# Hybrid encoder layer: memory queries and half of the SSD gate of the first token group made feature-major by seven products

## The chip, the cores and the metric

The kernel runs on one core of a Trainium2 chip. The metric is the device time of one execution in microseconds (us); lower is better. Before the change it is 1805.97 us, the median of 3 runs (1805.81 to 1807.87).

## The reference, cut to what matters

One layer of an encoder runs over 1280 tokens (1024 of a sample, 256 of a prompt), 2048 features wide, in fp32.

```python
hn = rms_norm(x, norm_g)
proj = hn @ w_in                                   # 2048 -> 4896 columns
xbc, z_ssd, dt_raw, q, k, v, z_att, mq, z_mem = split_cols(proj, IN_SIZES)
...
y = (y_f + y_b + d_skip[:, None] * xs)             # SSD, forward and backward
yg = (y * silu(z_ssd)).reshape(b, T, 2, 512)       # the SSD gate, two groups of 512 columns
o_ssd = rms_norm(yg, ...)
...
mq = rms_norm(mq.reshape(b, T, 4, 128), mq_norm_g) # memory queries, 4 heads of 128
sm = einsum('bthd,bmhd->bhtm', mq, mk) * 128 ** -0.5
o_mem = einsum('bhtm,bmhd->bthd', softmax(sm), mv) * silu(z_mem)
...
return x + concat([o_ssd, o_att, o_mem]) @ w_out
```

## The kernel before, in words

Tokens go in tiles of 128; tiles 0 to 4 are the first group (640 tokens), tiles 5 to 9 the second. Every large product is made in three matmuls: both operands are split into a high and a low fp32r part (`xH`/`xL` of the activations, `wh`/`wl` of the weights, `wsplit`, lines 200 to 204: ScalarE makes `wh`, VectorE `wl`), and high*high, high*low and low*high are summed in PSUM.

There are three forms of a large product:

- `block_tok` (lines 230 to 262) makes 512 columns **token-major** (tokens on partitions): for each of 16 slices k of the 2048 features, 5 token tiles with 3 matmuls of 512 columns each, 240 matmuls in all.
- `block_feat` (lines 264 to 298) makes 256 columns **feature-major** (columns on partitions): 192 matmuls of 320 tokens.
- `block_pair` (lines 1167 to 1198) makes 256 columns feature-major by a scheme of **seven products** of half-size blocks in place of eight: 7 products times 8 slices times 3 parts, 168 matmuls of 320 tokens. GpSimd forms the weights' sums ahead (`weight_sums`, line 1164, four operations per slice), ScalarE and VectorE split weights and sums, and `ev_seven` (lines 1264 to 1297) adds the seven results up. A unit is one such block of 256 columns.

The program runs in this order: memory keys and values; the attention queries `q` of group one; the **stage of seven products** with ten units for group one (gate of the attention `za`, gate of the memory part `zm`, and the six blocks x0 to x5 that feed the convolution); then `kv`, `mq`, `z0`, `z1` of group one, token-major; then everything of group two (x0 to x4, kv, x5, q, za, z0, z1, mq, zm); then the output product, first token-major for group one, then eight seven-product units for group two.

The many small pieces (norms, attention `attn`, memory attention `mem_attn`, the SSD passes `ssd_up` and `ssd_down`) are generators in two **lanes**. `run` (lines 1354 to 1376) drives a large product slice by slice; after each slice `pump` takes some steps off each lane, at the two rates that `RATES` (lines 32 to 34) gives for that block (for a feature-major block half of them, since its slices are half as long). A step stands in the program behind the slice at which it was taken. `need(fn, tiles)` runs a lane on at once until the named pieces are done. The leftovers of the seven products (taps of the convolution, gates) wait in the list `left`, and are taken by `some_left`.

What the change touches: `mem_attn` (lines 697 to 785) loads the queries `mq` of a tile, squares them (line 705), transposes them on TensorE into the PSUM tile `pmq` (line 713), splits the transposed ones (715, 717), and goes on to scores (`pms`, 730), transposes of the weights (`pmt`, 752) and values (`pmo`, 767). `ssd_down` (lines 991 to 1048) loads the gate `z` of a tile (line 1006), takes the part from the state (`pyb`, line 1022), multiplies by the gate (line 1026), and squares into the gate's own tile (line 1027); `turn_ssd` (line 986) transposes an earlier result into `pr`. `x_stats` and `stage_stats` sum the squares of the input rows. All small PSUM tiles share one ring of three, `mix`.

Of the kernel before, what the change touches and what calls it, by code (L numbers as in the profile page):

```python
# [19 lines left out]
P = 128  # L20
# [11 lines left out]
RATES = ({'kv': (2.0, 1.0), 'mq': (2.4, 1.6), 'z0': (2.2, 1.7), 'z1': (2.2, 1.7)},  # L32
         {'kv': (1.2, 1.5), 'x': (1.75, 1.85), 'q': (1.6, 2.5), 'za': (1.6, 2.5), 'z0': (1.55, 2.6),
          'z1': (1.55, 2.65), 'mq': (1.55, 2.8), 'zm': (1.55, 2.85), 'o': (1.95, 1.9)})
FAR = 1e30

UNITS = (0, 4, 1, 5, 2, 6, 7, 3, 8, 9)
# [6 lines left out]
def hymba_encoder_kernel(  # L44
# [62 lines left out]
    zT_d = [[dram([P, 4, 640], f"zT{c}_{g}") for g in range(2)] for c in range(2)]  # L107
    q_d = [dram([P, 512], f"q_{t}") for t in range(NT)]
    mq_d = [dram([P, 512], f"mq_{t}") for t in range(NT)]
    k_d = [dram([P, P], f"k_{t}") for t in range(NT)]  # L110
# [586 lines left out]
    def mem_attn(t):  # L697
# [4 lines left out]
        S.dma_start(q, mq_d[t])  # L702
        yield
        sq = w2("sq")
        A.activation(sq, q, AF.Square)
# [5 lines left out]
        ps = psum("pmq")  # L711
        for h in range(4):
            T.transpose(ps[:, h * P:(h + 1) * P].bitcast(F32R), qr[:, h * P:(h + 1) * P], identr)
# [3 lines left out]
        V.tensor_sub(ql, ps, qh.bitcast(F32))  # L717
# [273 lines left out]
    def ssd_down(t):  # L991
# [8 lines left out]
        for g in range(2):  # L1000
            c = slice(g * 512, (g + 1) * 512)

            y = mp.tile([P, 512], F32, tag="ya" if t % 2 else "rf", name="yd", bufs=2)
            S.dma_start(y, yp_d[t][:, c])
            z = mp.tile([P, 512], F32, tag="xs", name="zd", bufs=2)
            S.dma_start(z, z_d[g][t])
# [10 lines left out]
        for g in range(2):  # L1017
            c = slice(g * 512, (g + 1) * 512)
            y, z, st = ld[g]
            if not last:  # L1020
# [12 lines left out]
            if g == 0:  # L1033
                yield
# [229 lines left out]
    def ev_seven(kind, f0):  # L1264

        work, o = (conv_left, 2) if kind is None else (gate_left, 0)
# [35 lines left out]
    def gate_left(c, f0, rs):  # L1302
        th = []

        def tanhs():
            for r in rs:
                th.append(ev.tile([P, 640], F32, tag="evt", name="th"))
                A.activation(th[-1], r[:, :640], AF.Tanh, scale=0.5)

        def last(i):  # L1310
            V.scalar_tensor_tensor(out=th[i], in0=th[i], scalar=1.0, in1=rs[i][:, :640], op0=ALU.add, op1=ALU.mult)
            S.dma_start(zT_d[c][0][:, f0 + i, :], th[i])
        return [tanhs, lambda: last(0), lambda: last(1)]
# [27 lines left out]
    def x_stats(grp):  # L1341
        if grp == 0:
            yield from stats([(xrow(t), t) for t in range(5)],
                             lambda i: ev.tile([P, 512], F32, tag="evt" if i % 2 else "evu", name="xst"))
        else:
            yield from stats([(xrow(t), t) for t in (8, 9)],
                             lambda i: mp.tile([P, 512], F32, tag="xs" if i % 2 else "ya", name="xst", bufs=2))

    def stage_stats():

        yield from stats([(mrow(i), 10 + i) for i in range(4)] + [(xrow(t), t) for t in (5, 6, 7)],
# [127 lines left out]
    units = [(i // 2, i % 2 * 2) if i < 4 else (None, 2 * (i - 4)) for i in UNITS]  # L1479
# [44 lines left out]
    queue(1, x_stats, [1])  # L1524
# [30 lines left out]
    for b in range(5):  # L1555
        feat("x", b, ev_conv(1, 2 * b), 1, extra=one_left)
    need(attn, range(4))
    kv_shift()
    run(block_tok(w_kv, 5, ev_dtkv(5)), RATES[1]["kv"], extra=one_left)
    queue(0, k_prep, range(5, 10))  # L1560
    queue(0, attn, [4])
    queue(1, dt_prep, [5])
    feat("x", 5, ev_conv(1, 10), 1, extra=one_left)
# [3 lines left out]

    run(block_tok(w_in_rows("q"), 5, ev_raw(q_d, 5)), RATES[1]["q"], extra=when_done(2, lambda: queue(1, ssd_up, range(4, 8))))
# [108 lines left out]
```

## Time and profile before

| what | value |
|---|---|
| median of 3 runs | 1805.97 us |
| the profiled execution's own time | 1804.94 us |
| its span in the trace | 1803.2 us |
| TensorE matmul busy | 1791.4 us, 99% of the span |
| VectorE busy | 1210.3 us, 67% |
| ScalarE busy | 902.3 us, 50% |
| GpSimd busy | 456.6 us, 25% |
| granted TensorE clock | 1.0 |

The span is what lies between the first and the last instruction; 1.7 us of the execution lie around it. Matmuls overlap in the profile: a matmul's own duration is longer than the distance to the next one, so the sum of durations says nothing about what a matmul costs. The distance from start to start does.

### The profile page before, as it was taken

What the parts mean: (1) busy time and instruction counts of PE and PEld (TensorE: products, weight loads), DVE (VectorE), ACT (ScalarE), POOL (GpSimd) and SP (SyncE); (2) the same over time, 40 slices, a digit from 0 to 9 for tenths busy, and PEclk for the clock granted to TensorE, in tenths of its full rate; (3) what the DMA queues carried; (4) which work ended last, traced back from release to release, by engine and by line L of the source; (5) the groups of instructions that cost most, each with busy time, mean ns of one, the idle gap of its engine ahead of it and who ended that gap; (6) DMA issues with size and microseconds to landing.
All of it is one profiled execution on the core that took longest, in us unless ns stands there. A gap on an engine that the chain in (4) does not pass through costs nothing.

```text
span 1803.2 us, 30420 instructions
## 1 busy us (share of the span) xinstructions
PE 1791.4 (99%) x10546; PEld 1607.0 (89%) x10546; DVE 1210.3 (67%) x2303; ACT 902.3 (50%) x1999; POOL 456.6 (25%) x772
## 2 busy tenths in 40 slices
PE   9999999999999999999999999999999999999999
PEld 8789999999887799999989988887898888899999
DVE  5595788877657877675755766556775653867665
ACT  6554455444445756464435645544474533543332
POOL 0105888861110000000000001101100000058775
PEclk9999999999999999999999999999999999999999
DMA  8654454446544544344336355457785554644442
GB/s 299 190 178 122 137 151 152 126 134 217 168 134 152 177 133 139 121 132 133 118 95 192 113 164 173 128 181 233 230 269 162 180 189 142 215 154 147 141 144 79
DMA packets 198891, 290.58 MB, mean 161 GB/s; under 512 B 18960, under 2 KB 80464, under 8 KB 198736
## 3 DMA queue, kind: packets, MB, share of 16 engines
q1 hardware_dynamic: 198592, 288.57, 51.4%
q8 instruction: 83, 1.36, 0.3%
q14 instruction: 72, 0.59, 0.1%
q10 hardware_dynamic: 144, 0.06, 0.0%
HBM read 231.12 MB, written 57.44 MB: 160 GB/s over the span
## 4 chain that ended last, share of the span: by engine, by line
PE 87%; issue 5%; DMA 3%; DVE 2%; ACT 1%; POOL 1%; SPq 0%; ACTq 0%; DVEq 0%; POOLq 0%
PE acc L254 13%; PE acc L256 13%; PE acc L255 12%; PE acc L1194 6%; PE acc L1192 6%; PE acc L1193 6%; PE acc L289 5%; PE acc L290 4%; PE acc L291 4%; PE accm L1193 2%; PE accm L1192 2%; PE accm L1194 2%; PE py L924 2%; PE po L667 1%; PE ppt L657 1%
## 5 line engine op out<-in xcount | busy, mean ns | idle before, releaser
L203 DVE TENSOR_TENSOR wl<-wraw,wh 128x512 fp32r<-128x512 f32 (+1 forms) x480 | 340.5, 711 | 273.8 <-ACT wh L202 265.0
L254 PE MATMUL acc<-wh,xH 128*128 128x512 f32 (+1 forms) x1248 | 482.7, 387 | 0.2 <-ACT wh L202 0.2
L255 PE MATMUL acc<-wl,xH 128*128 128x512 f32 (+1 forms) x1248 | 472.2, 378 | 0.6 <-DVE wl L203 0.4
L256 PE MATMUL acc<-wh,xL 128*128 128x512 f32 (+1 forms) x1248 | 472.4, 379 | 0.0
L202 ACT ACTIVATE wh<-wraw 128x512 fp32r<-128x512 f32 (+1 forms) x480 | 293.4, 615 | 348.4 <-PE acc L256 189.5
L255 PEld LDWEIGHTS acc<-wl,xH 128*128 128x128 f32 x1248 | 234.9, 188 | 43.7 <-DVE wl L203 2.8
L254 PEld LDWEIGHTS acc<-wh,xH 128*128 128x128 f32 x1248 | 234.7, 188 | 43.6 <-issue 3.9
L256 PEld LDWEIGHTS acc<-wh,xL 128*128 128x128 f32 x1248 | 234.2, 188 | 43.4
L289 PE MATMUL acc<-xH,wh 128*128 128x320 f32 x640 | 203.9, 319 | 0.0
L290 PE MATMUL acc<-xL,wh 128*128 128x320 f32 x640 | 198.2, 310 | 0.0
L291 PE MATMUL acc<-xH,wl 128*128 128x320 f32 x640 | 198.0, 309 | 0.0
L202 ACT ACTIVATE sh<-ws 128x384 fp32r<-128x384 f32 x144 | 74.9, 525 | 180.9 <-POOL ws L1164 98.5
L203 DVE TENSOR_TENSOR sl<-ws,sh 128x384 fp32r<-128x384 f32 x144 | 100.1, 699 | 93.6 <-ACT sh L202 93.4
L1164 POOL TENSOR_TENSOR ws<-wraw 128x128 f32<-128x128 f32 x144 | 88.9, 617 | 202.5 <-DMA wraw<-in_w_in_pairs_dram 88.1
L629 POOL COPY lg<-nsink 128x2 f32<-128x2 f32 x40 | 16.5, 416 | 436.4 <-PE ppt L657 212.2
L289 PEld LDWEIGHTS acc<-xH,wh 128*128 128x128 f32 x640 | 120.3, 188 | 3.5 <-issue 2.7
L290 PEld LDWEIGHTS acc<-xL,wh 128*128 128x128 f32 x640 | 120.3, 188 | 2.3 <-issue 1.9
L291 PEld LDWEIGHTS acc<-xH,wl 128*128 128x128 f32 x640 | 120.2, 188 | 0.1
L1164 POOL TENSOR_TENSOR ws<-wraw,ws 128x128 f32<-128x128 f32 x144 | 94.6, 657 | 11.3
L358 DVE SCALAR_TENSOR_TENSOR c<-u,vec,c 128x638 f32<-128x638 f32 (+1 forms) x96 | 88.9, 931 | 11.2 <-ACT c L353 10.8
L1164 POOL TENSOR_TENSOR ws<-ws,wraw 128x128 f32<-128x128 f32 x144 | 93.3, 648 | 0.0
L1164 POOL TENSOR_TENSOR wraw<-wraw 128x128 f32<-128x128 f32 x144 | 89.1, 618 | 11.1
(426 smaller groups left out, 3601.3 us busy)
## 6 DMA issues: line engine op xcount, KB each, us to landing
wraw<-in_w_in_laid_dram SPq DMA_DIRECT2D x208, 256.0 KB, 2.8
wraw<-in_w_in_pairs_dram SPq DMA_DIRECT2D x80, 256.0 KB, 2.7
wraw<-in_w_out_laid_dram SPq DMA_DIRECT2D x64, 256.0 KB, 3.1
wraw<-in_w_out_pairs_dram SPq DMA_DIRECT2D x64, 256.0 KB, 2.8
rf<-ac SPq DMA_DIRECT2D x40, 256.0 KB, 3.6
rb<-ac SPq DMA_DIRECT2D x40, 256.0 KB, 4.0
wraw<-in_w_mem_laid_dram SPq DMA_DIRECT2D x32, 256.0 KB, 4.2
xst<-in_x_sample_dram SPq DMA_DIRECT2D x20, 256.0 KB, 4.9
```

The source lines that it names most:

```text
L202: a = A.activation(h, raw, AF.Copy)
L203: b = V.tensor_sub(l, raw, h.bitcast(F32))
L254: T.matmul(ps[t][:, :n], sh, h[:, :n], start=(k_ == 0), stop=False)
L255: T.matmul(ps[t][:, :n], sh, l[:, :n], start=False, stop=False)
L256: T.matmul(ps[t][:, :n], sl, h[:, :n], start=False, stop=(k_ == KT - 1))
L289: T.matmul(o, sh, cur["H", q][:, m, c], start=(k == 0), stop=False)
L290: T.matmul(o, sh, cur["L", q][:, m, c], start=False, stop=False)
L291: T.matmul(o, sl, cur["H", q][:, m, c], start=False, stop=(k == KT - 1))
L1164: G.tensor_tensor(out=o, in0=x, in1=y, op=op)
L1192: T.matmul(ps[p], h, xh, start=(k_ == 0), stop=False)
L1193: T.matmul(ps[p], h, xl, start=False, stop=False)
L1194: T.matmul(ps[p], l, xh, start=False, stop=(k_ == 7))
```

## The change

In words:

- Four more units go through the stage of seven products: y0 and y1, which are the two halves of `z0` (the SSD gate's first 512 columns), and m0 and m1, the two halves of `mq`, all for group one. The stage has 14 units now, in the order za0 x0 za1 x1 zm0 x2 zm1 x3 y0 x4 y1 x5 m0 m1. Their results are stored feature-major, in `yT` and `mT`.
- The token-major blocks `mq` and `z0` of group one are gone. Between the stage and group two stand `kv` and `z1` alone.
- `mem_attn` of tiles 0 to 4 loads a feature-major tile and turns it at its first step; it squares out of PSUM. The split then reads the loaded tile. The number of transposes is the same.
- `ssd_down` of tiles 0 to 4 loads the gate of the first 512 columns feature-major, and turns it with four transposes into the PSUM tile `pz`, which the multiplication reads and the square overwrites.
- The row sums of tiles 8 and 9 are taken in the stage of seven products.
- kv of group two comes after x5, not between x4 and x5; `mem_attn` of group one is queued before `z1`; the rates are new. In words of lane 0: z1 of group one 3.0 (before 2.2), x 2.1 (1.75), kv 1.4 (1.2), q 2.2 (1.6), za 2.05 (1.6), z0 2.0 (1.55), z1, mq and zm 1.9 (1.55); `o` is unchanged.

Core of the diff:

```diff
-RATES = ({'kv': (2.0, 1.0), 'mq': (2.4, 1.6), 'z0': (2.2, 1.7), 'z1': (2.2, 1.7)},
+RATES = ({'kv': (2.0, 1.0), 'z1': (3.0, 1.6)},
...
-UNITS = (0, 4, 1, 5, 2, 6, 7, 3, 8, 9)
+UNITS = (0, 8, 1, 9, 2, 10, 3, 11, 4, 12, 5, 13, 6, 7)
+PAIRS = ('za0', 'za1', 'zm0', 'zm1', 'y0', 'y1', 'm0', 'm1', 'x0', 'x1', 'x2', 'x3', 'x4', 'x5')
...
-        S.dma_start(q, mq_d[t])
-        yield
+        if grp == 0:
+            S.dma_start(hv(q, 4), mT_d[:, :, tc_])
+        else:
+            S.dma_start(q, mq_d[t])
+        yield
+
+        def turned():
+            ps = psum("pmq")
+            for h in range(4):
+                T.transpose(ps[:, h * P:(h + 1) * P].bitcast(F32R), qr[:, h * P:(h + 1) * P], identr)
+            return ps
+
+        tok_ = turned() if grp == 0 else q
         sq = w2("sq")
-        A.activation(sq, q, AF.Square)
+        A.activation(sq, tok_, AF.Square)
...
+        feat_ = q if grp == 0 else turned()
         qh = mp.tile([P, 512], F32R, tag="qT", name="mqh", bufs=2)
-        A.activation(qh, ps, AF.Copy)
+        A.activation(qh, feat_, AF.Copy)
...
+            if g == 0 and t < 5:
+                zr, z = z, psum("pz")
+                for j in range(4):
+                    T.transpose(z[:, j * P:(j + 1) * P].bitcast(F32R), zr[:, j * P:(j + 1) * P], identr)
...
+    def turned_left(dst, f0, rs):
+        def store():
+            for i in range(2):
+                S.dma_start(dst[:, f0 + i, :], rs[i][:, :640])
+        return [store]
...
-    run(block_tok(w_in_rows("mq"), 5, ev_raw(mq_d, 0)), RATES[0]["mq"],
+    queue(0, mem_attn, range(5))
+    run(block_tok(w_in_rows("z1"), 5, ev_gate(1, 0)), RATES[0]["z1"], refill_x(1),
         extra=when_done(1, lambda: queue(1, ssd_up, range(4))))
-    queue(0, mem_attn, range(5))
-    tok("z0", w_in_rows("z0"), ev_gate(0, 0))
-    tok("z1", w_in_rows("z1"), ev_gate(1, 0), refill_x(1))
...
-    for b in range(5):
+    for b in range(6):
         feat("x", b, ev_conv(1, 2 * b), 1, extra=one_left)
```

How it moves instructions on TensorE, at three places. The names: `ppt`, `po` are the transposed weights and the values of the attention, `py`, `pst`, `pyf` products of the SSD, `lg` the attention's weights, `acc` a large product.

First, the end of the attention of tile 3. Before, at the end of x2, the last six of its transposes stand alone behind a run of large matmuls, and the `po` that reads them follows after the 48 large matmuls that begin with the last two rows shown:

```order
L291 MATMUL acc<-xH_7170,wl 128x320
L657 MATMUL ppt<-identr,lg 128x128 x6
L924 MATMUL py<-xs,rb 128x64 x8
L289 MATMUL acc<-xH_7482,wh 128x320
L290 MATMUL acc<-xL_7483,wh 128x320
```

Now it stands at the start of kv of group two, where `need(attn, ...)` runs the lane to its end:

```order
L660 MATMUL ppt<-identr,lg 128x128 x9
L257 MATMUL acc<-wh,xH_6765 128x288
L660 MATMUL ppt<-identr,lg 128x128 x3
L862 MATMUL pst<-bh,bth 128x512
L863 MATMUL pst<-bl,bth 128x512
L864 MATMUL pst<-bh,btl 128x512
L879 MATMUL pyf<-state,bc 128x512
L670 MATMUL po<-pT,v_all 64x256 x6
```

Twelve transposes, a state product and the values now follow each other with one large matmul among them.

Second, the start of the memory attention of a tile. Before (tile 1, in x4), the transposes come a step after the square, which ScalarE took from the loaded tile:

```order
L850 MATMUL pst<-bh,bth 128x512
L851 MATMUL pst<-bl,bth 128x512
L852 MATMUL pst<-bh,btl 128x512
L713 MATMUL pmq<-identr,mq 128x128 x4
L289 MATMUL acc<-xH_6767,wh 128x320
```

Now (tile 0, in kv of group two) they are the first work on the loaded tile:

```order
L862 MATMUL pst<-fh,bth 128x512
L863 MATMUL pst<-fl,bth 128x512
L864 MATMUL pst<-fh,btl 128x512
L714 MATMUL pmq<-identr,mq 128x128 x4
L257 MATMUL acc<-wh,xH_6765 128x288
```

TensorE's row is the same; what it waits for is the load itself, no longer a load that ScalarE has already used.

Third, the backward SSD pass, at a tile of group one. Before, `pyb` opens the work on a tile:

```order
L667 MATMUL po<-pT,v_all 64x256 x4
L1022 MATMUL pyb<-state,cc 128x512
L986 MATMUL pr<-identr,yd 128x128 x4
L291 MATMUL acc<-xH_6933,wl 128x320
L289 MATMUL acc<-xH_6933,wh 128x320
```

Now the gate's transposes stand ahead of it:

```order
L259 MATMUL acc<-wh,xL_7087 128x512
L1039 MATMUL pz<-identr,zd 128x128 x4
L1042 MATMUL pyb<-state,cc 128x512
L998 MATMUL pr<-identr,yd 128x128 x4
L257 MATMUL acc<-wh,xH_7403 128x512
```

Four transposes and one more tile of the PSUM ring have come in, for each of five tiles.

More of the change, by code (lines that the diff above doesn't have):

```diff
@@ L1264, in ev_seven @@
     def ev_seven(kind, f0):
-        work, o = (conv_left, 2) if kind is None else (gate_left, 0)
+        work, o = (conv_left, 2) if kind is None else (turned_left if kind is mT_d else gate_left, 0)
         def begin(u):
@@ L1339, in stats, with x_stats @@
                 yield
[L1341 to L1347, printed above, removed]
+    def x_stats(_):
+        yield from stats([(xrow(t), t) for t in range(5)],
+                         lambda i: ev.tile([P, 512], F32, tag="evt" if i % 2 else "evu", name="xst"))
     def stage_stats():
-        yield from stats([(mrow(i), 10 + i) for i in range(4)] + [(xrow(t), t) for t in (5, 6, 7)],
+        yield from stats([(mrow(i), 10 + i) for i in range(4)] + [(xrow(t), t) for t in range(5, 10)],
                          lambda i: fin.tile([P, 512], F32, tag="xst", name="sst"), ahead=1, group=3)
@@ L1477, in hymba_encoder_kernel @@
         extra=lambda k: p_step(16 + k))
[L1479 removed]
+    dests = (zT_d[0][0], zT_d[1][0], yT_d, mT_d)
+    units = [(dests[i // 2], i % 2 * 2) if i < 8 else (None, 2 * (i - 8)) for i in UNITS]
     squares = stage_stats()
@@ L1553, in one_left, with gate @@
             some_left()
-    for b in range(5):
+    for b in range(6):
         feat("x", b, ev_conv(1, 2 * b), 1, extra=one_left)
+    def gate(name, c, after=None):
+        for b in range(2):
+            feat(name, b, ev_gateT(c, 1, 2 * b), 1, after if b else None)
     need(attn, range(4))
     kv_shift()
-    run(block_tok(w_kv, 5, ev_dtkv(5)), RATES[1]["kv"], extra=one_left)
+    run(block_tok(w_kv, 5, ev_dtkv(5)), RATES[1]["kv"], extra=lambda k: some_left() if left else None)
     queue(0, k_prep, range(5, 10))
```

35 lines of the change are left out of this document (17 added, 18 removed).

## The prediction

> **What bounds the kernel now.** I read the page first, then the chain that ended last, then TensorE's waits, then the stretches on both sides of the place that changes.
>
> ```profile
> span 1803.2 us, 30420 instructions
> ...
> PE 1791.4 (99%) x10546; PEld 1607.0 (89%) x10546; DVE 1210.3 (67%) x2303; ACT 902.3 (50%) x1999; POOL 456.6 (25%) x772
> ...
> PE 87%; issue 5%; DMA 3%; DVE 2%; ACT 1%; POOL 1%; SPq 0%; ACTq 0%; DVEq 0%; POOLq 0%
> ```
>
> TensorE is busy for 99% of the span and makes up 87% of the chain; no other engine is above 67%. A busy share of overlapping matmuls could still hide waits, so the waits come next (engine, what waited, for what: us in all, times, longest).
>
> ```profile
> PE pmt L752 <- DVE mpr L744: 1.5, 2, 0.9
> PE warm L1458 <- DVE zero L1456: 1.3, 1, 1.3
> PE psc L635 <- ACT qT L619: 1.0, 1, 1.0
> PE acc L1194 <- DVE wl L203: 0.9, 2, 0.6
> PE ppt L657 <- DVE nm L637: 0.8, 2, 0.5
> PE pxs L843 <- ACT pT L658: 0.6, 1, 0.6
> PE po L667 <- ACT pT L658: 0.6, 1, 0.6
> PE acc L255 <- DVE wl L203: 0.4, 2, 0.2
> PE acc L1192 <- ACT qs L322: 0.3, 1, 0.3
> PE acc L254 <- ACT wh L202: 0.2, 1, 0.2
> ```
>
> All of TensorE's waits come to 7.6 us, and those in the lanes' work (pmt, psc, ppt, pxs, po) to 4.5. So the time is the sum of what TensorE is given, in every stage. A change of its work counts one for one, as long as the other engines keep up. Next, the stretches (width; then busy us of PE, PEld, DVE, ACT, POOL; granted clock; DMA share; GB/s): the stage of seven products, then kv with mq of group one, then z0 with z1, then x0 to x4.
>
> ```profile
> 155.00:395.00 240.00, 239.08 (x1633) 238.45 (x1633) 193.43 (x291) 124.27 (x248) 200.63 (x310) 1.00 0.45 136
> ```
> ```profile
> 399.40:492.00 92.60, 92.60 (x535) 82.29 (x534) 62.53 (x138) 38.23 (x88) 12.36 (x29) 1.00 0.60 189
> 492.00:632.00 140.00, 138.90 (x697) 112.49 (x695) 99.08 (x207) 84.14 (x209) 13.99 (x25) 1.00 0.52 157
> 632.00:822.00 190.00, 189.08 (x1314) 180.24 (x1314) 134.75 (x289) 108.99 (x258) 9.06 (x15) 1.00 0.43 132
> ```
>
> The clock is 1.00 throughout. In the stage of seven products VectorE is at 81% and GpSimd at 84%: covered, with some 4 us in 24 to spare. Behind it VectorE is at 68%, 71% and 71%.
>
> **The change, term by term.** First the two blocks that go. Token-major matmuls of 512 columns, start to start:
>
> ```profile
> 119.76 0.39 PE L254 MATMUL acc<-wh,xH 128*128 128x512 f32 x1
> ...
> 121.12 0.39 PE L254 MATMUL acc<-wh,xH 128*128 128x512 f32 x1
> ```
>
> Six steps lie between these rows: 1.36 / 6 = 0.2267 us each. Two blocks of 240 matmuls: 480 x 0.2267 = **-108.8 us**.
>
> The four units that come. The first result of each unit is copied out at one and the same place of the unit, so the distance of these copies is the whole period of a unit, its waits and its edges included:
>
> ```profile
> L1282 ACT ACTIVATE yu<-acc x10: 417/430/439, 171.8 to 394.4; 128x320 f32<-128x320 f32 x10
> ```
>
> 222.6 us over nine periods is 24.73 us a unit. Four units: **+98.9 us**. With 168 matmuls that is 0.147 us each; a 320-column matmul costs 0.46 us per thousand columns against 0.44 of the 512-column one, so the shape is a little dearer, and the saved eighth outweighs it. The cover holds: GpSimd's 20.7 us and VectorE's 19.9 us per 24.7 us unit (84% and 81%) are those of the mixture that stands there already, and the new units need less of VectorE than a convolution unit (no taps).
>
> [...]
>
> The turning of the gate: 20 transposes. The transposes of the memory queries are of the same kind (row of the first, and of what starts behind it):
>
> ```profile
> 753.55 0.49 PE L713 MATMUL pmq<-identr,mq 128*128 128x128 f32 x4
> 753.87 0.51 PE L843 MATMUL pxs<-identr,xc 128*128 128x128 f32 x4
> ```
>
> 0.32 us for four: five times that is **+1.6 us**. The queries' own transposes only change their place. TensorE's work is thus -108.8 + 98.9 + 1.6 = **-8.3 us**.
>
> Edits at nothing: 32 slices of weights are loaded in either form, each 256 KB; four feature-major stores per 512 columns take the place of five token-major ones; the row sums of tiles 8 and 9 lie in a stage where ScalarE has 116 us of 240 free. They cost only where the DMA queue holds a weight load back, and the DMA share there is 0.45. The multiplication by a gate in PSUM lies on VectorE, off the path.
>
> **What the new order adds in waits.** Four places, each bounded.
>
> (a) The end of the attention of tile 3 is run in one piece ahead of kv of group two: twelve transposes into a ring of three PSUM tiles, which ScalarE must empty, then `po`, which needs all four copies.
>
> ```profile
> L658 ACT ACTIVATE pT<-ppt 128x384 f32<-128x384 f32 x48 | 20.8, 482 | 3.5 <-PE ppt L657 3.3
> ```
>
> Four copies are 1.9 us; three products stand beside them. Between 0 and 1.9; I take 1.2, nearer the upper end, since one large matmul alone is left for cover.
>
> (b) The turning of the queries waits for the load itself; behind it on TensorE stand the large matmuls of kv and q. ScalarE's square waited for this load before, at no cost to TensorE:
>
> ```profile
> L702 SPq DMA_DIRECT2D mq<-mq x10: 417/424/2237, 734.3 to 1477.9; - x10
> L713 PE MATMUL pmq<-identr,mq 128*128 128x128 f32 x40 | 5.1, 250 | 0.0
> L705 ACT ACTIVATE sq<-mq 128x512 f32<-128x512 f32 x10 | 6.3, 632 | 13.4 <-DMA mq<-mq 13.4
> ```
>
> Ten loads cost ScalarE 13.4 us, 1.3 each; five such on TensorE are 6.7 us. On the other side, the first load is issued at 734.3 and its transposes run at 753.55, 19 us later. Between 0 and 6.7; I take 0.4, since the load stands far ahead in its queue.
>
> (c) The gate's load stays three steps ahead of its first use, which is now `pz` on TensorE and no longer VectorE's multiplication; between 0 and as much as in (b); I take 0.
>
> (d) The lanes' steps of two blocks must find room elsewhere; all rates behind are up by a fifth to a third. If the lane waits grow in step, 4.5 us become 5.9: +1.4. They could also all go (-4.5). The upper end is VectorE's. Its work in kv to z1 is 62.5 + 99.1 = 161.6 us. Of it go 32 splits and five gates:
>
> ```profile
> L203 DVE TENSOR_TENSOR wl<-wraw,wh 128x512 fp32r<-128x512 f32 x448 | 325.9, 730 | 249.7 <-ACT wh L202 240.9 <-DMA wraw<-in_w_in_pairs_dram 3.0 <-DMA kr<-k 1.6
> L305 DVE SCALAR_TENSOR_TENSOR zs<-zs,acc x10: 666/686/689, 548.0 to 633.4; 128x512 f32<-128x512 f32 x10
> ```
>
> 161.6 - 32 x 0.730 - 5 x 0.686 = 134.8 us, in a stretch that shrinks to 232.6 - 108.8 = 123.8: 11 us too much if all of it stayed. It doesn't stay; the lanes run on into the x blocks, which take a fifth more steps per slice. There VectorE's 134.75 us hold 40 weight splits (0.730) and 40 taps:
>
> ```profile
> L358 DVE SCALAR_TENSOR_TENSOR c<-u,vec,c 128x638 f32<-128x638 f32 (+1 forms) x96 | 88.9, 931 | 11.2 <-ACT c L353 10.8
> ```
>
> 134.75 - 29.2 - 37.2 = 68 us of lane work and edges; a fifth more is 14. So 11 + 14 = 25 us of VectorE's work are squeezed in from z1 to x5, where it has 55 us free in the x blocks. I take the +1.4, since a stretch with VectorE at 86% had next to no wait:
>
> ```profile
> 560.00:632.00 72.00, 70.90 (x359) 55.65 (x357) 62.26 (x131) 50.70 (x125) 7.96 (x14) 1.00 0.52 160
> ```
>
> **The sum.** -8.3 + 1.2 + 0.4 + 1.4 = **-5.3 us**. The profiled execution took 1804.94 us (1803.2 of span, 1.7 around it), so 1799.6 against itself; it lies 1.0 us under the median of the runs shown, from which -5.3 makes **1800.7 us**.
>
> **The rivals.**
>
> *The gain is eaten* by waits of 4.7 to 11.9 us, from (a), (b) and (d) together at about their middles. For it: z1 of group one runs its lane a third faster while VectorE also refills the activations for group two. Against it: every wait of that sort was under 2 us before. It gives 1802.4 to 1809.6, about 1805.
>
> *VectorE becomes the bound from z1 to x5.* The splits `wl` then come late behind lane work in VectorE's queue, and the large matmuls wait for them. Of the 25 us two thirds exposed are +16.7: 1805.97 - 8.3 + 16.7 = about 1814, slower. It decides from 11.9 us (48% of the 25) on. For it: 134.8 us of work against 123.8. Against it: `wl` is four slices ahead, and its waits are 1.3 us in the whole run.
>
> *The seven products don't shorten the work*, because a matmul can't go faster than its weights load. The row is
>
> ```profile
> L255 PEld LDWEIGHTS acc<-wl,xH 128*128 128x128 f32 x1248 | 234.9, 188 | 43.7 <-DVE wl L203 2.8
> ```
>
> and 672 x 0.188 - 108.8 + 1.6 = +19.1 us, 1825. [...] The ten units that stand there, 147 ns a matmul, speak against it: loads overlap.
>
> **How the numbers follow.** The forecast, with waits from -1.5 to +4.7, gives 1796.2 to 1802.4 and has 0.61. The eaten gain has 0.25, VectorE as the bound 0.12, the weight load 0.02. About 0.2% (3.6 us) is what a measurement of this kernel can tell from no change; so faster 0.61, same 0.25, slower 0.14. The range reaches from the forecast's lower edge through most of the second case: 1796 to 1808.
>
> **What would show it.** Right: 14 units with copies 24.7 us apart; `pz` in five groups of four, 0.3 us each; kv of group one beginning near 498 us in place of 399; TensorE's lane waits at 5 to 8 us; no long wait of a large matmul for `wl`. Wrong: units over 25 us (GpSimd or VectorE late in the stage); waits of `acc` for `wl` or of large matmuls behind `pmq` for the load `mq`; VectorE over 95% for tens of us between z1 and x5. The sum is wrong by as much as these waits exceed 3 us.

## The result, and the profile after

The changed kernel takes 1802.67 us (median of 15 executions, 1800.25 to 1805.08); the kernel before, run beside it, takes 1806.84 us (15 executions, 1804.29 to 1809.17). The ratio is 0.9978, 95% interval 0.9970 to 0.9986: 4.2 us less, a little over the 0.2% that can be told from no change, with an interval that lies on both sides of 0.2%. The profiled execution took 1802.35 us, with a span of 1800.6.

The page of the kernel after, the same three lines as of before:

```profile
span 1800.6 us, 31167 instructions
...
PE 1786.7 (99%) x10758; PEld 1618.2 (90%) x10758; DVE 1247.4 (69%) x2358; ACT 911.1 (51%) x2029; POOL 546.1 (30%) x900
...
PE 85%; issue 5%; DMA 4%; DVE 3%; ACT 2%; SPq 1%; POOL 0%; ACTq 0%; DVEq 0%; POOLq 0%
```

It is the same picture: TensorE is busy for 99% of the span and makes up most of the chain. VectorE has risen from 67% to 69% and GpSimd, which forms the weights' sums of four more units, from 25% to 30%. Now TensorE's waits (us in all, times, longest):

```profile
PE pmk L447 <- issue: 2.1, 1, 2.1
PE warm L1480 <- DVE zero L1478: 1.3, 1, 1.3
PE acc L257 <- DVE yt L409: 0.9, 1, 0.9
PE acc L257 <- ACT mkr L419: 0.8, 1, 0.8
PE pmt L764 <- DVE mpr L756: 0.7, 2, 0.5
PE acc L258 <- DVE wl L206: 0.7, 3, 0.2
PE pacs L556 <- DVE w L545: 0.6, 1, 0.6
PE psc L638 <- DVE nm L640: 0.6, 1, 0.6
PE psc L638 <- ACT pz L1047: 0.5, 1, 0.5
PE acc L257 <- ACT wh L205: 0.5, 2, 0.3
PE pms L742 <- ACT mqh L727: 0.4, 1, 0.4
```

The first line is new: the transposes `pmk` of the memory keys wait 2.1 us in one piece, a wait for which the prediction has no term. The stretches (columns as in the prediction): the stage of seven products; z1 of group one; x0 to x5.

```profile
155.00:495.00 340.00, 339.81 (x2322) 339.19 (x2322) 273.50 (x405) 171.36 (x342) 289.40 (x442) 1.00 0.48 143
...
530.00:595.00 65.00, 62.30 (x291) 51.38 (x291) 57.32 (x117) 34.04 (x78) 7.87 (x13) 0.97 0.63 196
595.00:830.00 235.00, 234.70 (x1616) 220.86 (x1616) 181.41 (x405) 143.09 (x354) 20.33 (x31) 1.00 0.45 131
```

TensorE is as full as before in the stage and in the x blocks; VectorE is at 80% there (before 81%) and at 77% (before 71%). The loss that shows here stands in z1: 2.7 us without a matmul in 65, and a mean granted clock of 0.97 where the kernel before had 1.00 in each stretch.

**Where the time went, stage by stage.** The borders are starts of matmuls: the first of the stage of seven products, the first behind it (399.4 before, 497.9 after), and the first of the output's units (1602.1 and 1599.6). The middle holds everything token-major and all of group two.

| us | opening | seven products | middle | output units to the end |
|---|---|---|---|---|
| before | 151.8 | 247.7 | 1202.7 | 201.1 |
| after | 153.2 | 344.7 | 1101.7 | 201.0 |
| difference | +1.4 | +97.0 | -101.0 | -0.1 |

The table explains the 2.6 us between the two profiled executions (1804.94 and 1802.35 us), not the 4.2 between the medians. The opening has the same work in both kernels; its +1.4 us is what one execution differs from another there (149.0 to 153.2 us over all kernels below). The forecast had +98.9 for the stage and -108.8 + 1.6 + 3.0 = -104.2 for the middle. So the units came out 1.9 us cheaper, and the middle is 6.2 us longer than its own work says, in place of 3.0: 1101.7 - (1202.7 - 108.8 + 1.6) = 6.2. **Middle excess** below means this difference, worked out for each kernel from its own blocks. Two traces of the kernel after give 6.2 and 7.5 us (e1 below), so a difference of 1 us between two kernels says nothing.

The excess is not all waits. The middle of before, of after, and of e9, the fastest kernel below:

```profile
399.43:1602.12 1202.69, 1197.86 (x6880) 1042.52 (x6879) 785.99 (x1645) 616.79 (x1459) 96.65 (x182) 1.00 0.53 164
```
```profile
497.89:1599.59 1101.70, 1095.00 (x6421) 956.21 (x6419) 745.79 (x1589) 578.72 (x1396) 97.73 (x178) 1.00 0.55 166
```
```profile
495.02:1593.55 1098.53, 1094.43 (x6420) 955.00 (x6419) 744.99 (x1589) 578.90 (x1396) 101.90 (x178) 1.00 0.54 166
```

Width less TensorE's busy time is its idle time: 4.8 us before, 6.7 after, 4.1 in e9. So waits make up 1.9 of the 6.2 (2.1 at `pmk`, while all others together went from 4.8 to 4.6), and a stretch of half clock makes up 1.6 (below). The other 2.7 us lie in time in which the profile has TensorE busy; no run here shows what makes them.

**The wait in z1, instruction by instruction.** The timeline of the kernel after, first the load of the last memory-key tile (SyncE's queue), then what follows from it:

```profile
560.46 0.38 SPq L429 DMA_DIRECT2D mkr<-mr  x1
```
```profile
565.99 0.72 ACT L435 ACTIVATE sq<-mkr,rx 128x512 f32<-128x512 f32 x1 [1.80 <-DMA mkr<-mr]
...
566.74 0.69 DVE L436 TENSOR_REDUCE ss<-sq 128x4 f32<-128x512 f32 x1 [1.48 <-ACT sq L435]
...
567.52 0.56 POOL L123 TENSOR_SCALAR r<-ss 128x4 f32<-128x4 f32 x1 [21.34 <-DVE ss L436]
...
568.16 1.01 POOL L124 TENSOR_TENSOR r<-r,mhalf 128x4 f32<-128x4 f32 x1
...
569.20 0.75 DVE L441 SCALAR_TENSOR_TENSOR mkr<-mkr,rx,r 128x512 f32<-128x512 f32 x1 [1.18 <-POOL r L124]
...
570.27 0.68 DVE L442 TENSOR_TENSOR mkr<-mkr,state 128x512 f32<-128x512 f32 x1
```

From the issue of the load to the end of the last VectorE operation are 10.5 us, and each engine in the row waits for the one before it. TensorE reaches the transposes at the end of the chain too early:

```profile
568.48 0.48 PE L855 MATMUL pxs<-identr,xc 128*128 128x128 f32 x4
571.05 0.63 PE L447 MATMUL pmk<-identr,mkr 128*128 128x128 f32 x4 [2.10 <-issue]
...
572.29 0.63 PE L257 MATMUL acc<-wh,xH 128*128 128x512 f32 x1
572.72 0.63 PE L258 MATMUL acc<-wl,xH 128*128 128x512 f32 x1
```

The word "issue" in the bracket hides VectorE: `mkr` ends at 570.95 and `pmk` starts at 571.05. And the wait has a second price. Behind it the large matmuls stand 0.43 us apart in place of 0.227: the clock record has 0.5 for 3.41 us from 572.11 on. That is 8 matmuls x 0.20 = 1.6 us more. One wait thus cost 3.7 us, more than half of the middle's 6.2. New small waits stand around 1450 to 1550 us (`pmt`, `pms`, `yt`, 1.8 us together), where the kernel before has none; in exchange others have gone.

The load and the transposes are six steps of the lane apart. At 3.0 steps a slice that is two slices of 15 x 0.227 = 3.4 us each; before, at 2.4 (the removed block mq, where this work stood), it was two and a half. That is the first theory: **the lane's rate in z1 leaves a chain of dependent steps too little time.** The rows of before, the load and the same transposes:

```profile
468.20 0.38 SPq L426 DMA_DIRECT2D mkr<-mr  x1
```
```profile
478.93 0.60 PE L444 MATMUL pmk<-identr,mkr 128*128 128x128 f32 x4
```

TensorE came 10.7 us after the load there; without the wait it would have come after 8.5 now. That is 2.2 us less. But the chain is longer too: VectorE's last operation ended 9.0 us after the load before (477.20) and 10.5 now, and the load alone took 5.4 us to land, 4.3 before. With the chain of before, the wait would have been about 0.5 us. So the rate is one part of the cause and the longer chain, most of it the load's later landing, is another; no run here parts them. The rival: the 3.7 us are one execution's bad luck, or the loss lies in no place of its own but in many small waits, and a collision will turn up somewhere wherever the lanes move.

### The profile page after: what moved, and what is told of

Its sections match the earlier page's. It is cut to its first block, busy times and chain, and to the rows that moved or that the text cites. A ratio compares the mean times of both kernels' runs of the same rounds, so it can differ in the third digit from the quotient of the medians.

```text
span 1800.6 us, 31167 instructions
## 1 busy us (share of the span) xinstructions
PE 1786.7 (99%) x10758; PEld 1618.2 (90%) x10758; DVE 1247.4 (69%) x2358; ACT 911.1 (51%) x2029; POOL 546.1 (30%) x900
## 4 chain that ended last, share of the span: by engine, by line
PE 85%; issue 5%; DMA 4%; DVE 3%; ACT 2%; SPq 1%; POOL 0%; ACTq 0%; DVEq 0%; POOLq 0%
PE acc L257 9%; PE acc L259 9%; PE acc L258 9%; PE acc L1214 7%; PE acc L1212 7%; PE acc L1213 7%; PE acc L292 5%; PE acc L293 5%; PE acc L294 5%; PE accm L1213 3%; PE accm L1212 3%; PE accm L1214 3%; PE py L936 2%; PE po L670 1%; PE ppt L660 1%
## 5 line engine op out<-in xcount | busy, mean ns | idle before, releaser
L257 PE MATMUL acc<-wh,xH 128*128 128x512 f32 (+1 forms) x1088 | 418.9, 385 | 2.2 <-DVE yt L409 0.9
L258 PE MATMUL acc<-wl,xH 128*128 128x512 f32 (+1 forms) x1088 | 411.7, 378 | 0.8 <-DVE wl L206 0.7
L259 PE MATMUL acc<-wh,xL 128*128 128x512 f32 (+1 forms) x1088 | 411.1, 378 | 0.0
L257 PEld LDWEIGHTS acc<-wh,xH 128*128 128x128 f32 x1088 | 204.8, 188 | 39.9 <-issue 2.6
L258 PEld LDWEIGHTS acc<-wl,xH 128*128 128x128 f32 x1088 | 205.0, 188 | 39.4 <-DVE wl L206 3.3
L259 PEld LDWEIGHTS acc<-wh,xL 128*128 128x128 f32 x1088 | 204.7, 188 | 38.0 <-issue 1.2
L206 DVE TENSOR_TENSOR sl<-ws,sh 128x384 fp32r<-128x384 f32 x176 | 123.8, 706 | 103.6 <-ACT sh L205 100.6
L1184 POOL TENSOR_TENSOR ws<-wraw 128x128 f32<-128x128 f32 x176 | 112.1, 637 | 207.7 <-DMA wraw<-in_w_in_pairs_dram 90.1
L1184 POOL TENSOR_TENSOR ws<-wraw,ws 128x128 f32<-128x128 f32 x176 | 116.9, 664 | 13.8
L1184 POOL TENSOR_TENSOR wraw<-wraw 128x128 f32<-128x128 f32 x176 | 111.8, 635 | 13.7
```

What stands on the lines that cost most here:

```text
L206: b = V.tensor_sub(l, raw, h.bitcast(F32))
L257: T.matmul(ps[t][:, :n], sh, h[:, :n], start=(k_ == 0), stop=False)
L258: T.matmul(ps[t][:, :n], sh, l[:, :n], start=False, stop=False)
L259: T.matmul(ps[t][:, :n], sl, h[:, :n], start=False, stop=(k_ == KT - 1))
L1184: G.tensor_tensor(out=o, in0=x, in1=y, op=op)
```

## The experiments

Twelve kernels ran, four at a time on one chip, each time beside the kernel before: 1803.42 us there for e1 to e4, 1803.67 for e5 to e8, 1804.15 for e9 to e12. Times are given against the kernel before of the same chip.

### e1: the kernel after once more

No edit.

> The changed kernel once more, on the chip of the next three, for their comparison and for a second trace. Theory 1: the wait of 2.1 us ahead of the transposes of a memory-key tile in z1 of group one (the tile's load lands late, and ScalarE, VectorE and GpSimd follow each other behind it), with the half clock of 3.4 us behind it, belongs to the order of this kernel: it returns, between 1 and 3 us, with a stretch of half clock. Theory 2: it was a chance of that one execution: no wait over 1 us there, granted clock 1.0 from end to end. Time about 4 us under before with either.

Measured: 1800.86 us, -2.6 us, ratio 0.9983 (0.9974 to 0.9992). The wait is there again:

```profile
569.42 0.63 PE L447 MATMUL pmk<-identr,mkr 128*128 128x128 f32 x4 [1.92 <-issue]
```

The half clock follows again: the mean clock from 570 to 575 us is 0.66, which is 3.4 us at half. Beyond the profiled executions it can be counted only roughly: 3.41 us at half of 1800 make a mean clock of 0.999, and 11 of the 15 executions of after and 8 of the 11 here have 0.999; of the 63 of the kernel before that ran beside e1 to e12, one. (A 0.999 alone proves nothing: the profiled execution of e3 has it too, and its longest wait is 1.3 us, at the kernel's start.) So it is no single bad luck: the wait belongs to the kernel, and the half clock probably to most of its executions. The four later kernels that keep z1 at 3.0 and the load where it is (e6, e7, e8, e12) wait at this place as well, 1.84 to 3.07 us.

### e2: the load one tile ahead

```diff
     def mk_prep(i):
-        kr = w2("mkr")
-        S.dma_start(kr, mr_d[i])
+        if i == 0:
+            mk_load(0)
+        kr = mk_raw[i]
         yield
+        if i < 3:
+            mk_load(i + 1)
         yield
```

> The changed kernel with the load of each memory-key tile issued one tile ahead. Theory 1 (some 4 us of the forecast gain are lost to that one wait and the half clock behind it): 3 to 4 us faster than the changed kernel, about 8 us under before, and TensorE's waits in z1 of group one under 1 us. Theory 2 (the loss is spread over many small waits of the squeezed lanes): within 1 us of the changed kernel.

Measured: 1800.19 us, -3.2 us, ratio 0.9981 (0.9972 to 0.9990); 0.7 us under e1. The wait of `pmk` and the half clock are gone (clock 1.000 in all 11 executions). In z1 (530 to 595 us) TensorE waits elsewhere now:

```profile
PE acc L292 <- DVE zs L308: 1.3, 2, 0.9
PE pacs L565 <- DVE w L554: 0.6, 1, 0.6
```
```profile
530.00:595.00 65.00, 63.10 (x306) 52.19 (x305) 58.72 (x119) 35.10 (x79) 8.36 (x12) 1.00 0.64 200
```

The large matmuls of x0 wait for the gates `zs` with which z1 ends, late on VectorE. Middle excess 5.3 us, against 6.2 and 7.5 (after and e1). The first theory had expected 3 to 4 us from this edit; the second, within 1 us of the kernel after, has the time right. Yet the wait was real and is gone; with the rate left at 3.0, other waits of z1 took part of its place. Neither theory stands as it was put; the question is now whether it is the rate.

### e3 and e4: half of the change each

e3 makes only the queries by seven products; z0 stays token-major:

```diff
-UNITS = (0, 8, 1, 9, 2, 10, 3, 11, 4, 12, 5, 13, 6, 7)
+UNITS = (0, 8, 1, 9, 2, 10, 3, 11, 12, 13, 6, 7)
...
+    run(block_tok(w_in_rows("z0"), 5, ev_gate(0, 0)), RATES[0]["z0"],
...
+    tok("z1", w_in_rows("z1"), ev_gate(1, 0), refill_x(1))
```

e4 makes only the gate so; mq stays token-major:

```diff
-UNITS = (0, 8, 1, 9, 2, 10, 3, 11, 4, 12, 5, 13, 6, 7)
+UNITS = (0, 8, 1, 9, 2, 10, 3, 11, 4, 12, 5, 13)
...
+    run(block_tok(w_in_rows("mq"), 5, ev_raw(mq_d, 0)), RATES[0]["mq"],
```

In both, z1 of group one runs at 2.4 steps a slice and the blocks of group two at rates between those of before and after.

> Only the memory queries by seven products, the gate z0 token-major as before, rates between the old and the new ones. By the sum of TensorE's work: -54.4 + 49.5 = -4.9 us, no added transposes. If the work alone decides, about 4 to 5 us under before; if the lost cover costs most (theory 2), half as much cover is lost, and waits are fewer than in the whole change, so the gain is equal to or larger than that of the whole change per us saved. If the units are dearer than computed: within 1 us of before.

> Only the gate's first 512 columns by seven products, the memory queries token-major as before, rates between the old and the new ones. By the sum: -54.4 + 49.5 + 1.6 = -3.3 us. If the turning costs more than its 20 transposes (a slot of the PSUM ring held until the square is done), 1 to 2 us less than that.

Measured: e3 1798.75 us, -4.7, ratio 0.9974 (0.9966 to 0.9983); e4 1798.35 us, -5.1, ratio 0.9973 (0.9962 to 0.9984). Each half gains more than the whole did on this chip, by 2.1 and 2.5 us of medians, though the intervals overlap. e3 came as its sum says (-4.9); e4 gained more than its -3.3, which its interval still holds. z1 in both (530 to 595 us), e3 first:

```profile
530.00:595.00 65.00, 65.00 (x326) 54.47 (x325) 48.49 (x91) 37.44 (x90) 10.87 (x13) 1.00 0.67 214
```
```profile
530.00:595.00 65.00, 65.00 (x326) 54.45 (x325) 47.81 (x91) 37.60 (x89) 10.57 (x13) 1.00 0.64 209
```

Not a tenth of a microsecond of TensorE is lost, and VectorE has 48 us of work there in place of 57. The transposes `pmk` stand in the block ahead of z1, at 2.2 steps a slice, and do not wait. The middle excess is -0.6 and -0.5 us: the two halves of the sum hold, without any added wait. The waits belong to the whole, in which one token-major block less lies between the stage and group two, and the lane's steps of it have to go into what is left. Since these kernels have lower rates as well as one block more, they do not say which of the two it is.

### e5: z1 at 2.3 steps a slice, x at 2.4

```diff
-RATES = ({'kv': (2.0, 1.0), 'z1': (3.0, 1.6)},
-         {'kv': (1.4, 1.5), 'x': (2.1, 2.15), 'q': (2.2, 2.5),
+RATES = ({'kv': (2.0, 1.0), 'z1': (2.3, 1.6)},
+         {'kv': (1.4, 1.5), 'x': (2.4, 2.15), 'q': (2.2, 2.5),
```

With the load of e2 one tile ahead; so have e9, e10 and e11.

> The kernel after, with the load of each memory-key tile one tile ahead (as in the run e2) and the steps of the lane per slice in z1 of group one lowered from 3.0 to 2.3; x of group two takes 2.4 in place of 2.1, so that the steps not made in z1 are made there. Theory 1 (the squeeze of z1 is the loss: three steps a slice there leave VectorE late for the gates): the 2.3 us after z1 that were left in e2 go to under 1, and the time is 1 to 2 us below the e2 kind of kernel, that is 5 us below the kernel before on the same chip, ratio about 0.997. Theory 2 (the loss is spread over many small waits wherever lanes run faster): what z1 gains, x gives back, and the ratio stays at 0.998, 3 to 4 us below the kernel before.

Measured: 1799.33 us, -4.3 us, ratio 0.9974 (0.9964 to 0.9984). In z1 one wait of 0.6 us is left, and TensorE is busy for 64.27 of 65 us. But from 1353.9 us on, in the token-major blocks of group two, the list of waits has

```profile
PE pmt L773 <- DVE mpr L765: 2.5, 1, 2.5
```

and 6 of 8 executions have a clock of 0.999 (median 1800.1 us; the two with 1.000 took 1796.2 and 1798.8). The half clock is not in the profiled execution. What z1 gained, the lane lost again where it was pushed ahead. That x gives back what z1 gains is what the second theory had said; the time, -4.3 us, lies between the two theories (3 to 4, and 5). It could be chance of this one pair of rates; e9 and e10 ask that.

### e6: two units more, and e7: one token-major block more

```diff
-UNITS = (0, 8, 1, 9, 2, 10, 3, 11, 4, 12, 5, 13, 6, 7)
+UNITS = (0, 8, 1, 9, 2, 10, 3, 11, 4, 12, 5, 13, 6, 7, 6, 7)
```
```diff
     queue(0, mem_attn, range(5))
+    run(block_tok(w_in_rows("mq"), 5, ev_raw(mq_d, 0)), (0, 0))
     run(block_tok(w_in_rows("z1"), 5, ev_gate(1, 0)), RATES[0]["z1"], refill_x(1),
```

> The kernel after, with the two last units of the seven products (features of the memory queries, both pairs) done a second time, so that the stage has 16 units. Theory 1 (the stage costs its matmuls and nothing else; the term +98.9 of the sum holds): 2 x 24.64 = 49.3 us above the kernel after, so 45 to 47 us above the kernel before. Rival (units of plain copies at the end of the stage are cheaper, which would explain why the stage came 1.8 us under the forecast): under 48 us above the kernel after. Other rival (GpSimd or VectorE late when units follow one another without convolutions): over 51.

> The kernel after, with one token-major block of the memory queries of group one added ahead of z1, with no lane steps beside it; its output tensor is not read by group one. Theory 1 (a block costs its 240 matmuls of 512 columns: 240 x 0.2267): 54.4 us above the kernel after, 50 to 52 us above the kernel before, and so 5.1 us more than the two units of the same features in the run beside it. Rival (a block costs more than its matmuls, with its edge and its copies, and the removed blocks gained more than the sum says): 56 us or more. Other rival (the extra block pulls apart what collides in z1, and some of the lost waits go): under 53.

Measured: e6 1851.93 us, +48.3, ratio 1.0263 (1.0249 to 1.0277); e7 1852.46 us, +48.8, ratio 1.0265 (1.0251 to 1.0279). Against the kernel after (-2.6 us on the other chip) that is about 51 for each, so they did not come out 5.1 us apart: e6 is some 1.6 us dearer than the first theory, and e7 3 us cheaper, as its second rival had it (under 53). The traces say why. The stage of e6 takes 394.0 us, 49.3 more than that of after, to the tenth what two units were to cost. But its middle takes 1105.9 us, 2.9 to 4.2 us more than in e1 and after, though it holds the same work. `pmk` waits still longer, and some 6.8 us of half clock follow (a mean of 0.57 over the 8 us below), twice as much as in after. A second wait, of 2.1 us, stands at `ppt`, and the mean clock of the whole, 0.997 over 1851.2 us, stands for 9 to 13 us of half clock:

```profile
617.89 1.09 PE L447 MATMUL pmk<-identr,mkr 128*128 128x128 f32 x4 [3.07 <-issue]
```
```profile
616.00:624.00 8.00, 6.11 (x18) 4.98 (x19) 7.35 (x16) 1.18 (x3) 0.74 (x3) 0.57 0.57 183
```

The middle of e7 takes 1152.1 us, 49.1 to 50.4 more than in e1 and after for 54.4 us of matmuls. Its profiled execution has no half clock, which is 1.6 us, and TensorE idles 4.5 us in its middle in place of 7.5 and 6.7; with these added, the block comes to 53.8 and 54.2. `pmk` itself still waits 1.84 us. In the added block, which has no lane steps, VectorE is busy for 19.26 of 55 us:

```profile
506.00:561.00 55.00, 55.00 (x321) 49.52 (x320) 19.26 (x44) 12.87 (x27) 2.93 (x5) 1.00 0.40 118
```

So both prices of the sum hold, and work that is added elsewhere moves the waits and half clocks of the crowded middle by several microseconds either way.

### e8: group two at the rates of before

```diff
-         {'kv': (1.4, 1.5), 'x': (2.1, 2.15), 'q': (2.2, 2.5), 'za': (2.05, 2.5), 'z0': (2.0, 2.6),
-          'z1': (1.9, 2.65), 'mq': (1.9, 2.8), 'zm': (1.9, 2.85), 'o': (1.95, 1.9)})
+         {'kv': (1.2, 1.5), 'x': (2.1, 2.15), 'q': (1.6, 2.5), 'za': (1.6, 2.5), 'z0': (1.55, 2.6),
+          'z1': (1.55, 2.65), 'mq': (1.55, 2.8), 'zm': (1.55, 2.85), 'o': (1.95, 1.9)})
```

> The kernel after, with the lane's steps per slice of the blocks of group two as in the kernel before (kv 1.2, q and za 1.6, z0, z1, mq and zm 1.55), z1 of group one and x of group two as in the kernel after. Theory 1 (the squeeze of z1 is the loss, the raised rates behind it cost nothing): the same within 1 us as the kernel after, as long as the lanes are done ahead of the output blocks; what is left over runs there at 1.95 steps a slice. Theory 2 (the raised rates spread small waits over the blocks of group two): 1 to 3 us faster than the kernel after in the stretch of q to zm. Rival of both (the lanes are too late and the output block has to wait for them): 5 us or more slower, with waits of TensorE on the lanes behind the last block.

Measured: 1805.47 us, +1.8, ratio 1.0008 (0.9999 to 1.0017). The gain is gone. The lanes come late, and the loss stands in the output block (1490 to 1560 us):

```profile
PE acc L257 <- DVE yt L409: 1.7, 3, 0.7
PE pmq L714 <- DMA mq<-mq: 0.8, 1, 0.8
PE pmt L764 <- DVE mpr L756: 0.4, 1, 0.4
PE acc L258 <- DVE wl L206: 0.3, 1, 0.3
```

From 1500 to 1560 us TensorE is busy for 56.65 of 60 us, and for 59.11 in the kernel after (e8 first):

```profile
1500.00:1560.00 60.00, 56.65 (x295) 45.36 (x295) 39.44 (x83) 30.16 (x62) 2.49 (x4) 1.00 0.60 191
```
```profile
1500.00:1560.00 60.00, 59.11 (x265) 47.95 (x264) 37.47 (x67) 27.54 (x48) 1.12 (x3) 1.00 0.59 176
```

This is the rival of both theories, at 4.4 us above e1 in place of the 5 it named. The raised rates of kv to zm thus cost nothing that e8 gives back; they are needed. Of the rates, those of z1 and of x are left, which e9 and e10 try.

### e9 and e10: z1 lower, x raised less

e9 has 2.3 for z1 and 2.22 for x; e10 has 2.0 and 2.27.

```diff
-RATES = ({'kv': (2.0, 1.0), 'z1': (2.3, 1.6)},
-         {'kv': (1.4, 1.5), 'x': (2.4, 2.15),
+RATES = ({'kv': (2.0, 1.0), 'z1': (2.3, 1.6)},
+         {'kv': (1.4, 1.5), 'x': (2.22, 2.15),
```

z1's 16 slices make 11 steps less (16 in e10). The rates were meant to give these back in the six blocks of x; but a feature-major slice takes only half of the rate, so the 96 slices give back 6 (8 in e10), and e5 gave back 14. At the end of x, 64 of the matmuls `po` are done in e9 and e10, 76 in the kernel after and 88 in e5. Ahead of kv, `need(attn, ...)` runs e9 and e10 to the point that the kernel after reaches there too.

> The kernel of the run e5 with x of group two at 2.22 steps a slice in place of 2.4, so that the lanes should stand about where those of the kernel after stand when x is done. Theory 1 (the loss is the squeeze of z1; what e5 lost again at 1353 us came from lanes that were pushed ahead by x): the wait for mpr of 2.5 us at 1353 us is under 1, no half clock, 6 us below the kernel before on the same chip, ratio about 0.9965. Theory 2 (each order of the lanes meets some collision of 2 to 3 us, wherever it moves): 3 to 4 us below the kernel before, with a wait of over 1.5 us at a new place.

> As e9, with z1 at 2.0 steps a slice and x at 2.27. Theory 1: the excess after z1, 1.5 us in e5, goes to under 0.8, and the time is that of e9 or up to 1 us below it, since nothing else of it stands in z1. Theory 2: 3 to 4 us below the kernel before, with a wait of over 1.5 us at a new place, another than that of e9.

Measured: e9 1796.27 us, **-7.9 us**, ratio 0.9959 (0.9946 to 0.9971); e10 1798.08 us, -6.1, ratio 0.9964 (0.9950 to 0.9977). All ten executions have a clock of 1.000. z1 of e9, its one wait and its window:

```profile
PE pk L513 <- ACT kh L505: 0.7, 1, 0.7
```
```profile
530.00:595.00 65.00, 64.23 (x317) 53.95 (x316) 59.84 (x114) 37.45 (x84) 7.06 (x10) 1.00 0.69 214
```

VectorE is fuller there than in the kernel after (92% against 88%), and TensorE waits less. So it was not VectorE's capacity that was short. The longest wait of e9 in the middle is 0.9 us. All that the first theory expected of e9 came, and nothing of the second. e10 is another matter: it waits 1.44 us at `pmk` again. The list names ScalarE (`rf`), but VectorE's last operation on `mkr` ended 0.15 us before the transposes, so it is the end of the same chain, late at 2.0 steps a slice and with the early load. Its time is 1.8 us above e9's, where the first theory had it equal or up to 1 us below; a wait of over 1.5 us, as the second had it, did not come either. So a lower rate does not by itself clear that place; what else makes the chain late there is open.

The middle excess is 3.0 us in e9 and 3.7 in e10, not told apart. What e9 against e2 shows, both with the early load, is that the lower rate of z1, with x at 2.22 in place of 2.1, takes TensorE's idle time in the middle from 6.6 to 4.1 us and the time from -3.2 to -7.9. The early load alone (e2) is not enough, nor is the early load with z1 at 2.3 and x at 2.4 (e5); z1 lowered with the load left where it was has not been run. e9 is the fastest kernel of this study; its interval lies beside that of e2 and overlaps those of e3, e4, e5 and e10.

### e11: the gate alone, with the load of e2

> The kernel of the run e4 (the gate alone from the seven products, the queries token-major) with the load of each memory-key tile one tile ahead. Both theories: e4 has next to no excess after z1 (0.5 us), so the earlier load gains nothing there: ratio 0.997, 5 us below the kernel before, within 1 us of e4. If it loses over 1.5 us instead, the earlier load itself collides with another transfer, and what it gained in e2 was more than the 0.7 us that the medians show.

The edit is that of e2, on e4. Measured: 1798.47 us, -5.7 us, ratio 0.9970 (0.9958 to 0.9981), middle excess 0.5 us against -0.5 in e4. As expected: where no wait stands at `pmk`, the early load gains nothing, and it does no harm that these runs can tell.

### e12: the gate turned six times

```diff
-                for j in range(4):
+                for j in [j for _ in range(6) for j in range(4)]:
```

> The kernel after with the four transposes of each gate tile made six times over, the last overwriting the earlier ones with the same values: 100 transposes more. Theory 1 (a transpose costs its 0.08 us of TensorE and nothing else, as the term +1.6 of the sum has it): 8 us above the kernel after, about 5 us above the kernel before, ratio 1.002 to 1.004. Rival (part of the transposes runs in gaps of TensorE that are there anyway): under 4 us above the kernel after. Other rival (behind them the gate's square holds a PSUM buffer, and each of the five places costs a wait): over 12.

Measured: 1806.25 us, +2.1, ratio 1.0013 (1.0004 to 1.0022); against the kernel after (-2.6) 4.7 us, between the 8 of the theory and the 4 of its rival. One place of turning in the kernel after, then in e12:

```profile
1235.27 0.46 PE L1039 MATMUL pz<-identr,zd 128*128 128x128 f32 x4
1235.57 1.09 PE L1042 MATMUL pyb<-state,cc 128*128 128x512 f32 x2
```
```profile
1233.57 2.17 PE L1039 MATMUL pz<-identr,zd 128*128 128x128 f32 x24
1235.57 1.09 PE L1042 MATMUL pyb<-state,cc 128*128 128x512 f32 x2
```

0.30 us for four, 2.00 for 24: the price of the sum is right, and five such places add 8.5 us of work. The middle grew by 4.8 to 6.1 us only. As in e7, part of the added work took the place of waits: behind 1200 us two waits are left in e12, of 0.6 and 0.5 us, where the kernel after has five, of 2.5 us together.

## Why the prediction was right, and where it was not

**TensorE's work, -8.3 us: right in its prices; the stage came out 1.9 us cheaper.** 1800.7 us was forecast and 1802.67 measured. Part of these 2.0 us is the start: the forecast began at 1805.97, and the kernel before, run beside the changed one, took 1806.84. The change itself is -4.2 us where -5.3 was forecast and, on the second chip, -2.6. The two prices that carry it were shown in their stages: two more units add 49.3 us (e6), and the halves' middles come out within 0.6 us of the 54.4 that a block was to give (e3, e4). The mis-sized term is "+98.9": it measured +97.0. The first and last copy of each kind of unit in the kernel after:

```profile
L1302 ACT ACTIVATE yu<-acc x14: 416/419/437, 173.1 to 492.8; 128x320 f32<-128x320 f32 x14
...
L1144 ACT ACTIVATE yu<-acc x8: 437/438/439, 1619.2 to 1791.8; 128x320 f32<-128x320 f32 x8
```

319.7 / 13 = 24.59 us, and 172.6 / 7 = 24.66 for the output's units, which have no leftovers beside them. A unit is 24.65 us, and the stage of 14 took 14 x 24.62. That of before took 10 x 24.77: about 1.2 us in it were waits that the price of 24.73 then multiplied, and that the longer stage did not have. The rival that a product cannot go faster than its weights load is out with this: 24.66 us / 168 = 147 ns again, not 188.

**pz, +1.6: right.** 0.30 us for four against 0.32 (rows in e12).

**(a), the burst ahead of kv of group two, +1.2: too dear.** The list of waits has none there. The twelve transposes and the values stand in TensorE's row as the order had it, from 826.32 to 831.24 us, with a large matmul, three state products and `pyf` among them, and these were cover enough.

**(b), `pmq` on the load, +0.4: the wait fell on another engine.**

```profile
L706 SPq DMA_DIRECT2D mq<-mT x5: 544/631/1661, 817.6 to 924.8; - x5
...
  DMA mq<-mT: 1.8, 2
```

The first load is issued at 817.6 and turned at 833.9 us, 16 us later. ScalarE's split `mqh` of the loaded tile, which has become the first reader, waited 1.8 us in two of five tiles; TensorE 0. **(c)**, 0, was 0 for the load; `psc` waits 0.5 us for the PSUM buffer that the gate's square now holds.

**(d), the squeezed lanes, +1.4: the step that failed.** It scaled the sum of the old small waits by the rates, and bounded the rest by VectorE's capacity from z1 to x5. The capacity was no bound: VectorE had 181.41 of 235 us in the x blocks, and TensorE's waits for `wl` are 0.7 us in all. What came was one chain of dependent steps over five engines, at the highest of the new rates and behind a load that took 1.1 us longer to land than before, and the half clock behind it: 3.7 us at one place, while all other waits of the middle stayed as they were (4.6 us in place of 4.8). The text had named that block ("z1 of group one runs its lane a third faster"), as evidence for the rival of the eaten gain; it had no price for a chain. The middle's 6.2 us in place of 3.0 already lie in that rival's 4.7 to 11.9, and 1802.67 us lies on the border of the two cases (1802.4). In the profiled pair the middle cost 3.2 us more than forecast, the opening 1.4 more and the units 1.9 less; that the total stayed within 3 us of the forecast is the luck of misses with opposite signs. The sign held, the working of (d) did not.

That the added waits hang on the rates is shown in part: with the early load and a lower rate in z1, TensorE has less idle time in the middle (4.1 us in e9) than in the kernel before (4.8). The 3.0 us of excess that e9 still has are thus no added waits; that they equal the 3.0 of the forecast is chance.

Open: why the opening, with the same work, takes 149.0 to 153.2 us; why the last load of a memory-key tile lands later in z1; and what the part of the excess is that is neither waits nor half clock (2.7 us in after, 3.8 in e9, where the waits have fallen). None was tried.

## What to carry to other kernels

A rate of background steps per slice is not only a throughput: it is the time that each step of a dependent chain has until the next one stands in TensorE's row. When a block is removed and its steps are moved, look for the longest chain (a load, a square, a reduction, a root, a scaling, a transpose: 9.0 us before and 10.5 after) and count the slices that cover it at the new rate, with the load's landing in the new place, before any engine's busy share. Taking away the one wait that the profile shows may only move it (e2, e5). Here the earlier load, a lower rate in z1 and lanes that were not pushed ahead behind x together gave the fastest kernel (e9).

## What the runs showed of the hardware

In the kernel after, a wait of TensorE of 2.10 us cost almost as much again behind its end, 1.6 us. The granted clock fell to 0.5 there for 3.41 us (0.50 from 572.11 to 575.52 us, 1.00 ahead of it and behind it). It fell so for 3.4 us behind waits of 1.92 us in e1 (0.66 over 570 to 575 us) and 2.67 in e12 (0.57 over 570 to 574 us), and for some 6.8 us behind e6's wait of 3.07 (0.57 over 616 to 624 us). Large matmuls stood 0.43 us apart in it, in place of 0.227. It did not fall in the profiled executions of e7 and e8, with waits of 1.84 and 1.89 us at the same instruction, nor in that of e5, with 2.47, though other executions of these three kernels have a clock of 0.999 (2 of 4, 6 of 11 and 6 of 8).

So the length of the wait alone does not decide: it fell behind 1.92 us in e1, and not behind 2.47 in e5. What else decides was not shown.
